# When a head's queries and keys are made ready: always ahead, or when their products are there

## The chip, the cores and the metric

One Trainium2 chip, one of its NeuronCores. The metric is device time in microseconds, the median of several executions of the same program.

## The reference, cut to what matters

Two transformer blocks, one after the other, on 512 tokens of width 1024. The first block is a feed-forward layer, a mixer, another feed-forward layer and a gated embedding; the second is a mixer with sparse attention and a mixture of 32 experts. The change lies in the first block's mixer, which has two kinds of attention side by side:

```python
u = rms_norm(h, g_mix[i]) @ w_in[i]
q_lat, kv_lat, k_rope, qd, kd, vd = jnp.split(u, IN_OFFSETS, axis=-1)
# diff_mixer, 4 heads, each with two pairs of q and k of width 64
q = rms_norm(qd.reshape(B, S, DIFF_HEADS, 2, DIFF_QK), g_q)
k = rms_norm(kd.reshape(B, S, DIFF_HEADS, 2, DIFF_QK), g_k)
a = a1 - lam * a2          # two softmaxes with a bias by distance
o = rms_norm(a @ v, g_sub) * (1.0 - lambda_init)
# mla_mixer, 8 heads: q and k come from normed latents by w_q_up and w_kv_up
h = h + jnp.concatenate([o_mla, o_diff], axis=-1) @ w_out[i]
```

## The kernel before

The program is written with a tile framework that adds waits and buffers. Products of the large weights are made with operands split in a high and a low half, three matmuls for one (lines 399 to 401; lines 651 to 653 where tokens stand on the partitions). A weight comes by a DMA of SP's queue; ScalarE writes its high half (line 376), VectorE or, for every other weight, GpSimd its low half (lines 379 and 383).

In the mixer of the first block two Python generators issue instructions in turns. `stream(tasks)` goes through the projections in the order of `TASKS1`: `qk1 v0 kv qk2 v1 ql0 ql1 rq qk3 kr ple0 rkv wkv krn mk mq0 mv ple1 mq1 wo2 wo3 wo0`. (`qk0` stands ahead of it.) `qk` makes the queries and keys of a diff head with their norms, `v` the values of two heads, `mk` and `mq` those of the MLA heads, `wo` is a quarter of the output projection, which waits for two finished heads, and `ple` belongs to the gated embedding. `attention()` goes through eight items in the order of `ITEMS1`: the diff heads d0 to d3, then the MLA pairs of heads m0 to m3. For each there are four steps:

- `prep` (`diff_n`, `mla_n`): TensorE turns the normed products (line 836), and ScalarE, VectorE and, for MLA, GpSimd write the high and low halves of queries and keys (lines 391 to 395, `dq`, `dk`, `mq`, `kt`). It first waits with `need` until the products are marked as there.
- `score` (`diff_s`, `mla_s`): score matmuls (line 414 for d, 399 to 401 for m), the row's extreme on VectorE (860, 962), exponentials on ScalarE (864, 964); for d, VectorE joins the two softmaxes (873, tile `ad`).
- `out` (`diff_o`, `mla_o`): TensorE turns the probabilities (1153), ScalarE or VectorE copies them (1155, 1157), and they are multiplied by the values (884, 986).
- `diff_f` for d: the last norm of a head's output (line 905).

`score` of a head is issued in turns with `out` of the head before it. Before the loop, two heads are made ready; inside it, each turn makes ready the head two ahead, gathered in `late`.

`merge` decides whose turn it is. Each `yield` of a generator names a cost, and `merge` keeps a sum for each, `t[0]` for attention and `t[1]` for tasks; `self.clock` follows the tasks' sum. With the weights `wa` and `wb` of the call, here 100.0 and 135.0:

```python
i = 0 if t[0] * w[1] <= t[1] * w[0] else 1
if g[i] is None or blocked == i and g[1 - i] is not None:
    i = 1 - i
```

A `yield None` (a `need` that isn't met) hands the turn to the other. A product is there at the clock of its `mark` plus a lag, 8.0 (`LAG`) for normed products and 1.0 for values. The costs sum to 137.9 for the tasks (a block of `qk` or `v` 11.2, `mq` 5.6, `mk` and `mv` 2.8, a projection 5.2, a `wo` 10.4) and to 99.6 for attention.

The order in which the generators issue is an order of priority: when the program is built, a scheduler can put a later instruction of an engine in front of one that it takes to be still waiting. On the chip each engine then keeps to the order that came out.

Of the kernel before, what the change touches and what calls it, by code (L numbers as in the profile page):

```python
# [28 lines left out]
NWM = 32  # L29
LAG = 8.0  # L30
ITEMS1 = "d0 d1 d2 d3 m0 m1 m2 m3"
TASKS1 = "qk1 v0 kv qk2 v1 ql0 ql1 rq qk3 kr ple0 rkv wkv krn mk mq0 mv ple1 mq1 wo2 wo3 wo0"
TASKS2 = "qi1 qi2 qi3 qa0 ka0 va0 qa1 ka1 va1 qa2 ka2 va2 qa3 ka3 va3 ckv qb0 ukv qb1 qb2 qb3 g00 g01 g02 g03 g04 g05 g06 g07 u00 u01 u02 u03 g10 g11 g12 g13 g14 g15 g16 g17"
LK, LQ, LA, LB = 1.0, 9.0, 3.0, 0.0
# [202 lines left out]
class Prog:  # L237
# [329 lines left out]
    def block1(self):  # L567
# [45 lines left out]
        done = {}  # L613
# [16 lines left out]
        def mark(key, lag=0.0):  # L630
            done[key] = self.clock + lag
# [39 lines left out]
        def evac(t, b, ps):  # L671
            with self.tc.high_priority(offset=HP1):
                for i in (0, 1):
                    c = slice(256 * i, 256 * i + 256)
                    nc.scalar.activation(t[:, c], ps[:, c], AF.Copy, scale=rx[0][:, 2 * b + i : 2 * b + i + 1])
# [21 lines left out]
        def values(v):  # L697
            def then(b, ps):
                t = self.U("vd")
                evac(t, b, ps)  # L700
                for h in (2 * v, 2 * v + 1):
                    for i in (0, 1):
                        vd[h, 2 * b + i] = t[:, 256 * i + P * (h % 2) : 256 * i + P * (h % 2) + P]
                    mark(("v", h), 1.0)
            return then

        rx = []
# [95 lines left out]
        def t_ple(w, half):  # L803
            for m4 in range(4):
                ps = self.G()
                self.gemm(ps, w, pT, 2, o=m4 * 256)
                y = self.U("pp")
                nc.scalar.copy(y, ps)
                self.sumsq(accp, y, len(pp) == 0)
                pp.append(y)  # L810
                yield 1.3
# [90 lines left out]
        def diff_f(h):  # L902
            y, rr = M_.pop(("f", h))
            t = self.U("on")
            nc.vector.scalar_tensor_tensor(t, y, gs[:, 3:4], self.bc1(rr), op0=OP.mult, op1=OP.mult)
            oT[4 + h] = self.HL(f"oT{4 + h}")
            self.split(oT[4 + h], t)
            yield 0.4
# [107 lines left out]
        for b in range(2):  # L1016
            T_[f"ple{b}"] = [(I["w_pp"][b], lambda w, b=b: t_ple(w, b))]
        tasks = sum((T_[n] for n in TASKS1.split()), [])
        score, out, prep = {"d": diff_s, "m": mla_s}, {"d": diff_o, "m": mla_o}, {"d": diff_n, "m": mla_n}

        def attention():
            items = [(n[0], int(n[1])) for n in ITEMS1.split()]
            fin = []
            late = []
            for kind, i in items[:2]:
                yield from prep[kind](i)
            for n, (kind, i) in enumerate(items):
                g = [score[kind](i)]
                if n:
                    g.append(out[items[n - 1][0]](items[n - 1][1]))  # L1030
                yield from self.zip_(*g)
                if fin:
                    yield from diff_f(fin.pop())
                if n and items[n - 1][0] == "d":
                    fin.append(items[n - 1][1])

                late += items[n + 2 : n + 3]
                if late and (late[0][0] == items[n + 1][0] or kind != items[n + 1][0] or len(late) > 1):
                    while late:
                        k2, i2 = late.pop(0)  # L1040
                        yield from prep[k2](i2)
            yield from out[kind](i)

        for _ in self.stream(lead):
            pass
        self.merge(attention(), self.stream(tasks), 100.0, 135.0)
        self.dump("oT", [t[:, 0, :].bitcast(F32) for t in oT])
        acc3 = self.U("acc3")
        xs = []
# [1207 lines left out]
```

## Time and profile before

| | |
|---|---|
| median of 3 runs | 2174.3 us (2173.36 to 2177.2) |
| the profiled execution, its own time | 2175.46 us |
| its span, first to last instruction | 2173.6 us |
| TensorE busy (PE) | 2094.4 us, 96% |
| weight loads of TensorE (PEld) | 1513.4 us, 70% |
| VectorE (DVE) | 949.0 us, 44% |
| ScalarE (ACT) | 734.7 us, 34% |
| GpSimd (POOL) | 536.6 us, 25% |
| mean granted clock of TensorE | 0.983 |

Busy is the share of the span in which an engine executes. PEclk is the granted clock of TensorE: 1.00 is 2.4 GHz, 0.50 is 1.2 GHz, and a value between them is a mean over a stretch with both. In a timeline row the bracket tells how long the engine had been idle and what it waited for. The matmuls overlap, so one lasts longer in a row than it is apart from the next.

### The profile page before, as it was taken

Reading aid. Unit: us, or ns where it says so; the run is one execution under the profiler, and the core shown is the slowest. Engines: PE = TensorE matmul, PEld = TensorE weight load, DVE = VectorE, ACT = ScalarE, POOL = GpSimd, SP = SyncE. Lnnn points to the kernel's source line nnn. Section 1 sums busy time; section 2 is a strip of 40 time slices with the busy share of each in tenths; the row PEclk is TensorE's granted clock in tenths of the full one; section 3 lists DMA queues with packets and bytes.
Section 4 is the critical chain, followed back from the end, with each engine's and each line's share of the span. In section 5 each row is a group of like instructions: output and inputs, shape, how many; then the busy total and the mean of one; then the engine's idle time right before and its main releaser. Section 6 shows DMA issues by size and latency. Waiting matters only on the chain.

```text
span 2173.6 us, 26063 instructions
## 1 busy us (share of the span) xinstructions
PE 2094.4 (96%) x10321; PEld 1513.4 (70%) x10321; DVE 949.0 (44%) x1671; ACT 734.7 (34%) x1233; POOL 536.6 (25%) x441
## 2 busy tenths in 40 slices
PE   8999999998799999999998999999999999999997
PEld 6888888875566788888877777667887455545544
DVE  4323234555565532332476995553253232323322
ACT  4213223444663422222443667442231111111112
POOL 3323234221520532323443445111230000000000
PEclk9999999999799999999999999999999999999999
DMA  4333333320101233333322101012626899999994
GB/s 162 97 94 92 96 97 107 119 69 30 39 20 38 79 98 97 97 97 97 103 89 78 49 30 54 30 46 71 230 69 243 353 398 415 420 409 406 416 395 161
DMA packets 67984, 331.01 MB, mean 152 GB/s; under 512 B 7808, under 2 KB 8976, under 8 KB 43792
## 3 DMA queue, kind: packets, MB, share of 16 engines
q1 hardware_dynamic: 67280, 328.24, 41.0%
q8 instruction: 83, 1.36, 0.3%
q10 hardware_dynamic: 576, 1.05, 0.1%
q14 instruction: 45, 0.37, 0.1%
HBM read 327.16 MB, written 2.10 MB: 151 GB/s over the span
## 4 chain that ended last, share of the span: by engine, by line
PE 82%; DVE 7%; ACT 5%; POOL 2%; issue 2%; DMA 0%; SPq 0%; DVEq 0%; ACTq 0%; POOLq 0%
PE pss L1820 10%; PE psg L399 9%; PE psg L401 9%; PE psg L400 9%; PE psg L1820 8%; PE pss L401 4%; PE pss L399 4%; PE pss L400 4%; PE pst L400 4%; PE pst L399 4%; PE pst L401 4%; PE pst L1820 4%; ACT whl L376 1%; PE psg L651 1%; PE psg L653 1%
## 5 line engine op out<-in xcount | busy, mean ns | idle before, releaser
L383 POOL TENSOR_TENSOR whl<-wraw,whl 128x512 fp32r<-128x512 f32 x228 | 304.3, 1356 | 626.8 <-ACT whl L376 414.5
L376 ACT ACTIVATE whl<-wraw 128x1024 fp32r<-128x1024 f32 (+1 forms) x227 | 237.0, 1045 | 618.7 <-PE psg L401 241.1
L379 DVE TENSOR_TENSOR whl<-wraw,whl 128x1024 fp32r<-128x1024 f32 (+1 forms) x113 | 156.9, 1388 | 64.2 <-ACT whl L376 64.0
L2120 POOL TENSOR_TENSOR fr<-fv,mhalf 128x1 f32<-128x1 f32 x4 | 2.2, 545 | 513.8 <-DVE fv L2119 512.1
L1820 PE MATMUL pss<-mw,xe 128*64 128x512 f32 x512 | 115.3, 592 | 0.0
L1820 PE MATMUL pss<-mw,hT 128*64 128x512 f32 x480 | 109.7, 611 | 0.6 <-ACT hT L1998 0.5
L1820 PE MATMUL psg<-mw,xe 128*64 128x512 f32 x480 | 108.2, 593 | 0.0
L524 POOL TENSOR_TENSOR t<-t,t 128x512 f32<-128x512 f32 x44 | 57.3, 1302 | 202.1 <-DVE t L523 189.7
L523 DVE TENSOR_TENSOR t<-pss,rb_f 128x512 f32<-128x512 f32 x44 | 30.4, 691 | 162.9 <-PE pss L401 162.9
L556 DVE SCALAR_TENSOR_TENSOR h<-pst,h 128x512 f32<-128x512 f32 x48 | 33.2, 692 | 140.2 <-PE pst L401 140.2
L2093 DVE TENSOR_TENSOR h<-h,psg 128x512 f32<-128x512 f32 x120 | 81.2, 687 | 22.8 <-PE psg L1820 22.8
L1980 DVE SCALAR_TENSOR_TENSOR mt<-pss,sc,mt 128x512 f32<-128x512 f32 x16 | 12.0, 751 | 179.1 <-PE pss L1820 178.5
L1820 PEld LDWEIGHTS pss<-mw,xe 128*64 128x64 f32 x512 | 36.7, 137 | 73.1 <-issue 73.1
L1820 PEld LDWEIGHTS psg<-mw,xe 128*64 128x64 f32 x480 | 34.4, 137 | 68.1 <-issue 64.8
L1820 PEld LDWEIGHTS pss<-mw,hT 128*64 128x64 f32 x480 | 33.9, 140 | 65.1 <-issue 61.1
L395 DVE SCALAR_TENSOR_TENSOR yel<-pss,sc,yeh 128x512 fp32r<-128x512 f32 x32 | 24.0, 751 | 121.5 <-ACT yeh L394 121.5
L1820 PE MATMUL pst<-disp,uhh 128*128 128x256 f32 x256 | 66.7, 287 | 1.2 <-DVE disp L1898 1.2
L521 DVE TENSOR_TENSOR t<-psg,rb_f 128x512 f32<-128x512 f32 x44 | 30.4, 691 | 81.6 <-PE psg L401 76.1
L1820 PE MATMUL pst<-disp,uhl 128*128 128x256 f32 x256 | 65.2, 281 | 0.0
L1979 ACT ACTIVATE mt<-psg,sc 128x512 f32<-128x512 f32 x16 | 11.0, 687 | 157.1 <-PE psg L1820 134.2
L394 ACT ACTIVATE yeh<-pss,sc 128x512 fp32r<-128x512 f32 x32 | 22.0, 687 | 115.2 <-PE pss L1820 105.0
L433 POOL TENSOR_TENSOR acc<-acc,sq 128x512 f32<-128x512 f32 x33 | 49.9, 1513 | 39.8 <-ACT sq L432 36.3
(938 smaller groups left out, 5693.8 us busy)
## 6 DMA issues: line engine op xcount, KB each, us to landing
mw<-in_w SPq DMA_DIRECT2D x188, 1024.0 KB, 9.4
wraw<-in_w_gu SPq DMA_DIRECT2D x87, 512.0 KB, 3.6
wraw<-in_w_d SPq DMA_DIRECT2D x48, 512.0 KB, 3.5
wraw<-in_w2A SPq DMA_DIRECT2D x38, 512.0 KB, 3.5
wraw<-in_w_inB SPq DMA_DIRECT2D x12, 512.0 KB, 3.5
wraw<-in_w_out SPq DMA_DIRECT2D x8, 512.0 KB, 3.5
wraw<-in_w_pg SPq DMA_DIRECT2D x8, 512.0 KB, 3.5
wraw<-in_w_up SPq DMA_DIRECT2D x8, 512.0 KB, 3.4
```

The source lines that it names most:

```text
L376: nc.scalar.activation(hl[:, 0, :n], raw[:, :n], AF.Copy)
L379: nc.vector.tensor_sub(hl[:, 1, :n], raw[:, :n], hl[:, 0, :n].bitcast(F32))
L383: nc.gpsimd.tensor_sub(hl[:, 1, c], raw[:, c], hl[:, 0, c].bitcast(F32))
L399: mm(ps, whi, xhi, start=first, stop=False)
L400: mm(ps, whi, xlo, start=False, stop=False)
L401: mm(ps, wlo, xhi, start=False, stop=last)
L433: (eng or nc.gpsimd).tensor_add(acc, acc, t)
L521: nc.vector.tensor_tensor(t1, pg, rb, op=OP.mult)
L524: nc.gpsimd.tensor_tensor(t2, t1, t2, op=OP.mult)
L556: nc.vector.scalar_tensor_tensor(self.h[m], py, 0.5, self.h[m], op0=OP.mult, op1=OP.add)
L1820: return self.next_to(nc.tensor.matmul(*args, **kw))
L2093: self.nc.vector.tensor_tensor(self.h[m], self.h[m], ps, op=OP.add)
```

## The change

The loop of `attention()` is written anew. Only the first head is made ready before it. In a turn, where the head to be scored isn't ready yet, it is made ready then, followed by a `yield` of the new constant `GAP`, 2.5, which issues nothing; in the first turn, head 1 is made ready too if its products are there. At the end of a turn, heads up to two ahead are made ready, but only while `there` says that their products are marked and due by the clock. `there` asks and doesn't wait. The weights of `merge` become 118.0 and 138.0. `values` marks the values of its two heads when its second half is issued, no longer after the first half too.

```diff
--- before.py
+++ after.py
@@ -29,6 +29,7 @@
 NWM = 32
 LAG = 8.0
 ITEMS1 = "d0 d1 d2 d3 m0 m1 m2 m3"
+GAP = 2.5
 TASKS1 = "qk1 v0 kv qk2 v1 ql0 ql1 rq qk3 kr ple0 rkv wkv krn mk mq0 mv ple1 mq1 wo2 wo3 wo0"
 TASKS2 = "qi1 qi2 qi3 qa0 ka0 va0 qa1 ka1 va1 qa2 ka2 va2 qa3 ka3 va3 ckv qb0 ukv qb1 qb2 qb3 g00 g01 g02 g03 g04 g05 g06 g07 u00 u01 u02 u03 g10 g11 g12 g13 g14 g15 g16 g17"
 LK, LQ, LA, LB = 1.0, 9.0, 3.0, 0.0
@@ -701,7 +702,8 @@
                 for h in (2 * v, 2 * v + 1):
                     for i in (0, 1):
                         vd[h, 2 * b + i] = t[:, 256 * i + P * (h % 2) : 256 * i + P * (h % 2) + P]
-                    mark(("v", h), 1.0)
+                    if b:
+                        mark(("v", h), 1.0)
             return then
 
         rx = []
@@ -1021,10 +1023,26 @@
         def attention():
             items = [(n[0], int(n[1])) for n in ITEMS1.split()]
             fin = []
-            late = []
-            for kind, i in items[:2]:
+            rope = [True]
+
+            def there(kind, i):
+                return all(key in done and self.clock >= done[key] for key in ([("qk", i)] if kind == "d" else ["mk", ("mq", i // 2)]))
+
+            def ready(kind, i):
                 yield from prep[kind](i)
+
+            yield from ready(*items[0])
+            made = 1
             for n, (kind, i) in enumerate(items):
+
+
+                if made == n:
+                    yield from ready(*items[n])
+                    made += 1
+                    yield GAP
+                elif n == 0 and there(*items[1]):
+                    yield from ready(*items[1])
+                    made += 1
                 g = [score[kind](i)]
                 if n:
                     g.append(out[items[n - 1][0]](items[n - 1][1]))
@@ -1033,17 +1051,14 @@
                     yield from diff_f(fin.pop())
                 if n and items[n - 1][0] == "d":
                     fin.append(items[n - 1][1])
-
-                late += items[n + 2 : n + 3]
-                if late and (late[0][0] == items[n + 1][0] or kind != items[n + 1][0] or len(late) > 1):
-                    while late:
-                        k2, i2 = late.pop(0)
-                        yield from prep[k2](i2)
+                while made < min(n + 3, len(items)) and there(*items[made]):
+                    yield from ready(*items[made])
+                    made += 1
             yield from out[kind](i)
 
         for _ in self.stream(lead):
             pass
-        self.merge(attention(), self.stream(tasks), 100.0, 135.0)
+        self.merge(attention(), self.stream(tasks), 118.0, 138.0)
         self.dump("oT", [t[:, 0, :].bitcast(F32) for t in oT])
         acc3 = self.U("acc3")
         xs = []
```

## Rows read from the trace of the kernel before

**Rows 1.** The page: busy times, and TensorE in 40 slices of the span.

```profile
PE 2094.4 (96%) x10321; PEld 1513.4 (70%) x10321; DVE 949.0 (44%) x1671; ACT 734.7 (34%) x1233; POOL 536.6 (25%) x441
PE   8999999998799999999998999999999999999997
```

**Rows 2.** Busy time by stage: us, engines (count), PEclk, DMA.

```profile
405.04:417.30 12.26, 12.26 (x107) 12.26 (x106) 5.22 (x10) 5.79 (x11) 2.56 (x2) 1.00 0.25 87
417.30:431.87 14.57, 14.35 (x83) 10.62 (x81) 10.01 (x33) 8.01 (x16) 2.54 (x2) 1.00 0.21 72
431.87:451.77 19.90, 19.90 (x169) 19.90 (x168) 10.25 (x22) 10.64 (x21) 5.10 (x4) 1.00 0.24 81
451.77:478.85 27.08, 26.59 (x139) 19.22 (x137) 18.63 (x55) 15.17 (x32) 2.73 (x3) 1.00 0.15 44
505.81:528.86 23.05, 17.09 (x77) 9.78 (x76) 14.08 (x50) 11.13 (x27) 1.27 (x1) 0.90 0.05 18
528.86:549.98 21.12, 14.49 (x54) 7.61 (x53) 14.56 (x48) 9.56 (x23) 2.69 (x3) 0.82 0.09 26
549.98:575.22 25.24, 20.89 (x71) 16.26 (x72) 10.37 (x26) 17.06 (x32) 9.25 (x8) 0.70 0.00 0
621.76:640.17 18.41, 17.54 (x94) 11.41 (x93) 13.65 (x24) 9.05 (x22) 2.51 (x2) 1.00 0.06 22
640.17:661.10 20.93, 17.88 (x95) 11.97 (x94) 12.62 (x20) 12.44 (x28) 5.40 (x4) 0.92 0.00 0
```

**Rows 3.** The fourth stage, line 651 alone, then line 401 alone.

```profile
451.77:478.85 27.08, 2.56 (x9) 1.70 (x9) 1.00 0.15 44
451.77:478.85 27.08, 6.63 (x16) 3.02 (x16) 1.00 0.15 44
```

**Rows 4.** The same columns in two shorter stretches.

```profile
524.00:528.00 4.00, 2.67 (x11) 1.76 (x9) 1.03 (x3) 1.33 (x4) 0.00 (x0) 0.52 0.00 0
548.00:560.00 12.00, 10.57 (x36) 8.34 (x35) 4.96 (x15) 4.46 (x9) 4.06 (x4) 0.50 0.00 1
```

**Rows 5.** Timeline of TensorE: start us, us, what, [idle before].

```profile
427.08 0.40 PE L401 MATMUL psg<-xs2h,whl 128*128 128x512 f32 x1
429.40 0.40 PE L399 MATMUL psg<-xs6h,whl 128*128 128x512 f32 x1
451.77 1.04 PE L836 MATMUL pst<-ident,y 128*128 128x128 f32 x8
505.81 1.03 PE L836 MATMUL pst<-ident,y 128*128 128x128 f32 x8
513.84 0.50 PE L414 MATMUL pss<-dkh,dqh 64*128 64x512 f32 x1 [1.06 <-DVE mn L860]
521.87 0.49 PE L414 MATMUL pss<-dkh,dqh 64*128 64x512 f32 x1 [1.57 <-DVE mn L860]
547.23 2.08 PE L884 MATMUL psg<-at,vd 128*128 128x512 f32 x2 [5.52 <-ACT at L1155]
587.00 1.33 PE L836 MATMUL pst<-ident,ym 128*128 128x128 f32 x5 [1.17 <-DVE ym L668]
594.17 0.50 PE L401 MATMUL pss<-kth,mql 128*128 128x512 f32 x1 [1.74 <-POOL mql L392]
621.76 1.28 PE L836 MATMUL pst<-ident,ym 128*128 128x128 f32 x8
```

**Rows 6.** Timeline of VectorE and GpSimd.

```profile
508.41 0.75 DVE L395 SCALAR_TENSOR_TENSOR dkl<-pst,g,dkh 128x512 fp32r<-128x512 f32 x1 [0.35 <-ACT dkh L394]
512.42 0.75 DVE L873 SCALAR_TENSOR_TENSOR ad<-sb,cf 128x512 f32<-128x512 f32 x1
541.97 2.49 POOL L383 TENSOR_TENSOR whl<-wraw,whl 128x512 fp32r<-128x512 f32 x2 [10.38 <-ACT whl L376]
543.29 1.72 DVE L873 SCALAR_TENSOR_TENSOR ad<-sb,cf 128x512 f32<-128x512 f32 x1
625.75 2.51 POOL L392 TENSOR_TENSOR mql<-mqn,mqh 128x512 fp32r<-128x512 f32 x2 [9.12 <-ACT mqh L391]
```

## The prediction

> **What bounds the kernel now.** I read the page first: TensorE is busy 96% of the span, no other engine half of it, and its 40 slices stand at 9 but for a dip in the tenth and eleventh (489 to 598 us) [rows 1]. That dip is the first block's attention, which is all the change touches; before and behind it only time moves. I then cut this stretch by stages [rows 2]. The reader is to see two kinds. In the dense kind (405 to 479 us) VectorE and ScalarE are half busy, and whenever a score waits, projection matmuls stand ready: in the 27.08 us from 451.77 TensorE idles 0.49. In the sparse kind the same attention work stands with hardly anything beside it: from 505.81 TensorE idles 5.96 of 23.05, from 528.86 6.63 of 21.12, from 549.98 4.35 of 25.24, with a granted clock down to 0.70 [rows 2]. So the limit is local: TensorE's own work in one place, a chain through VectorE and ScalarE in the other. The timeline of TensorE shows that chain: score pairs at 513.84 and 521.87 with one pair between, 4.0 us a pair, each having waited for VectorE's L860 [rows 5].
>
> Call one head's scores with the outputs of the head before it a bundle. Walking through the merge's arithmetic with the code's costs gives the order of before, and the trace agrees. d0's scores alone and then d1's with d0's outputs stand in the dense place (417 and 452 us); at tasks' time 80.4, when d3's products come due, two bundles stand one behind the other (505.81 and 528.86): d2 with d1's outputs, d3 with d2's. The cause is the loop: it wants head n+1 made ready before head n is scored, so all scores stand one head late, behind the wait for products.
>
> **What the change does to the order.** The same walk with the new loop: d0's scores go to task time 8.4 instead of 19.6; d1's scores and d0's outputs to 19.6 and 23.7 instead of 47.2; d2 with d1's outputs to 47.2 instead of 80.4; only d3 with d2's outputs stays at 80.4. At 101.1, m0 is scored after its own preparation alone; m1's preparation comes behind that bundle, and m1's bundle now before mq1 and wo2, not behind them. m2 is prepared at 115.8 and scored at once, as is m3. The later marking of v costs nothing: it keeps d0's outputs from asking for values not issued yet.
>
> The pause gives no cover. A pause adds 2.5 to attention's time, and tasks come next only if that then exceeds 118/138 of theirs. At the five pauses (task times 19.6, 47.2, 80.4, 101.1, 115.8) the allowance is 16.8, 40.4, 68.7, 86.4, 99.0; attention stands at 7.3, 19.5, 32.1, 45.1, 75.3 behind the pause. It is never ahead. The new ratio binds first in m3's bundle, at 99.0, and the old one did there too (85.8). I cost pause and ratio at nothing; were there cover, it would be tasks between preparation and score.
>
> **The sum.** *Sparse place.* Two bundles and the last 12 ple0 matmuls take 505.81 to 549.98, 44.17 us [rows 2]. One remains. From above, the first bundle's 23.05 plus the 12 matmuls uncovered: ten stand 2.32 us apart end to end [rows 5], 0.232 each, 2.8, so 25.9. From the other side, the second bundle's 21.12, which held these 12, plus the preparation chain no longer done ahead, from the transposes at 505.81 to the end of the last low half at 508.41 + 0.75 = 509.16 [rows 5, 6], 3.35, so 24.5. I take 25.2: saved 19.0.
>
> *Dense place.* The bundle moved there costs what a bundle costs among projections. The stage from 451.77 holds one, with 9 matmuls of line 651, which is a third of its kind (lines 651 to 653), and 16 of line 401, a third of its own (399 to 401) [rows 3]: 27 and 48. The former stand 19.90/169 = 0.118 apart [rows 2]. So 27.08 - 27 x 0.118 - 48 x 0.232 - 1.04 for the transposes of a preparation [rows 5] = 11.7, plus 0.5 for half as many transposes in d0's finish, which moves too: 12.2. Cover is there for the waits of d1 and d2 on their fresh halves; without it each would cost up to 3.35. Net of both places: -6.8.
>
> *MLA heads.* Preparation in a join between two bundles is dearer than behind tasks: the stage from 640.17, with m3's preparation, idles 3.05, the one from 621.76, with m2's behind mq1 and wo2, 0.87 [rows 2]. There will be two such joins (m1, m3) instead of one: +2.2. m1's 12 transposes leave the half-clock place, where five took 1.33 (0.27 each), for one where eight take 1.04 (0.13) [rows 5]: -1.6. Then m1, m2 and m3 are scored at once, and the first score may wait for its low halves. From below 0, since the outputs of the head before fill in; from above the whole chain, 621.76 to the second mql at 628.26, 6.5 less 1.0 of transposes, 5.5 [rows 5, 6]. The one such wait shown, m0's, is 1.74 with GpSimd loaded [rows 5]; there GpSimd is busy only 2.5 to 5.4 us in some 20 [rows 2]. I take 0.6 each: +1.8. Together +2.4.
>
> *Clock.* At the end of the first sparse bundle the granted clock is 0.52 and from 548 to 560 us 0.50 [rows 4], the lower level of 1.2 GHz, after a wait of 5.52 on a ScalarE copy [rows 5]. The 10.57 us of matmuls there would take 5.3 less at 2.4 GHz. That is the upper bound of a gain if the chain behind is entered warm, nothing the lower: the first bundle too ended cold. I take 1.6.
>
> Preparing fewer heads ahead shortens the lives of tiles; no stage shows a wait for one, so nothing for that. DMA is busy 0.25 or less [rows 2]: nothing either. Sum: -6.8 + 2.4 - 1.6 = -6.0. The profiled execution took 2175.46 us (2173.6 of span and 1.9 around it), so 2169.5; it stands 1.2 above the median 2174.3, so 2168.3 as a median.
>
> One rule speaks against it. At 541.97 GpSimd splits a weight, and VectorE's `ad` at 543.29, beside it, takes 1.72 against 0.75 elsewhere [rows 6]. The Trainium skill (SBUF — State Buffer, section "SBUF: two separate sides") says that VectorE with two SBUF inputs and GpSimd take turns on one pair of ports, each for a whole instruction, and the trace agrees with its 1.72. By the row alone it is late once; by the rule every split that meets such an instruction does this.
>
> **Rivals.**
>
> *Fresh heads wait (the other side).* m1, m2 and m3 stop TensorE for their low halves, as m0 does at 594.17. At 4 us each, in the upper part of the bounds, that is 12 instead of 1.8: +4.2, 2178.5. It cancels the gain at 2.6 us each. For it: the pause places nothing between. Against it: 16 transposes and their output products of the head before are ready. 15 in 100.
>
> *The dense place is not free.* The moved bundle goes at its chain's 4.0 us a pair, 16 us instead of 12.2, because projection evacuations queue on ScalarE behind exponentials. Then -2.2, 2172.1, which would count as no change. For it: two bundles stand nearer there. Against it: 0.49 idle in the stage from 451.77. 25 in 100.
>
> *More than the sum.* The waits of the fresh heads vanish and the chain behind the sparse place runs warm: -6.8 + 0.6 - 5.3 = -11.5, 2162.8. 15 in 100.
>
> *Ports.* Eight weight splits stand in 405 to 452 us (2, 2 and 4) [rows 2]; if each meets the moved bundle's VectorE work and holds it 0.97 us uncovered, +7.8, so +1.8, 2176.1. Against it: TensorE is full there. 5 in 100.
>
> The sum itself has 40 in 100, with a range of its own of 2165.5 to 2171.
>
> **Numbers.** 0.2%, 4.3 us, is about what a measurement of this kernel can tell from no change. Faster: three quarters of the sum's 40, the 15 of more, 5 of the dense rival's: 0.50. Same: 10, 18 and 4 of the ports: 0.32. Slower: the 15 of the fresh heads and 3 over: 0.18. The range reaches from below the larger gain, 2161, to 2177, short of the fresh heads' time.
>
> **What would show it.** In the changed profile: one bundle between the last kr projection and the first kvlh matmul, which come 17 to 21 us closer together; stages before it longer by about 12 us and still full; GpSimd's mql as releaser of scores of m1 to m3, under 1 us each. Wrong if TensorE idles in the early stages, if the sparse place loses less than 15, or if the MLA stretch grows by over 6.

## The result, and the profile after

The changed kernel takes 2192.44 us (2191.54 to 2193.55, 4 runs) beside 2174.01 of the kernel before in the same series: a ratio of 1.0082, 95% interval 1.0065 to 1.0100. It is slower by 18.4 us, where 2168.3 was forecast, and lies outside the range. The profiled execution took 2193.55 us, its span is 2191.8.

Line numbers after are one higher in the helpers, two higher in the task code and 15 higher behind `attention()`: L860 is L862, L884 is L886, L836 is L838, L401 is L402, L1155 is L1170.

The page first: the busy line and TensorE's slices, to stand beside [rows 1].

```profile
PE 2104.9 (96%) x10321; PEld 1518.6 (69%) x10321; DVE 952.5 (43%) x1671; ACT 735.7 (34%) x1233; POOL 537.3 (25%) x441
PE   8999999988689999999999899999999999999998
```

TensorE executes the same 10321 matmuls and is busy 10.5 us longer, at a mean granted clock of 0.978 beside 0.983, so part of the loss is a slower clock. The dip, 87 in the tenth and eleventh slice before, is now 8868 from the ninth, which begins at 438 us and was full.

Next, three stretches in the windows view, of equal work in both kernels but for a few matmuls at the first edge (under 0.5 us): from 405 to the norm of the q latents, which ends the dense place (L442 before, L443 after, the matmul on `accq`); from there to the first `mk` matmul that waits for `ym`, the sparse place; from there to the norm that opens the next feed-forward layer, the MLA heads. Before:

```profile
405.00:484.87 79.87, 75.91 (x513) 64.61 (x511) 47.22 (x122) 42.31 (x84) 17.55 (x14) 1.00 0.21 69
...
484.87:565.28 80.41, 63.32 (x290) 44.67 (x290) 39.80 (x123) 36.31 (x78) 13.93 (x13) 0.83 0.09 31
...
565.28:731.03 165.75, 153.01 (x720) 110.96 (x721) 107.83 (x166) 95.64 (x186) 58.62 (x43) 0.96 0.12 39
```

After:

```profile
405.00:511.76 106.76, 93.96 (x570) 73.66 (x568) 61.00 (x172) 51.70 (x107) 17.71 (x15) 0.92 0.17 52
...
511.76:571.64 59.88, 47.27 (x230) 35.87 (x230) 26.31 (x73) 26.80 (x55) 13.74 (x12) 0.82 0.12 41
...
571.64:748.62 176.98, 158.53 (x720) 112.75 (x721) 111.65 (x166) 96.22 (x186) 58.85 (x43) 0.94 0.12 36
```

The sparse place gives back 80.41 - 59.88 = 20.5 us, as forecast. The dense place costs 26.9 instead of 12.2, the MLA heads 11.2 instead of 2.4. Net +17.6, nearly all of the 18.2 between the spans.

Where the dense place loses is plain in one window of after, 20 us of the places that were full before [rows 2]:

```profile
432.00:452.00 20.00, 11.82 (x44) 6.25 (x44) 12.47 (x45) 8.71 (x21) 2.53 (x2) 0.66 0.10 30
```

TensorE is idle 8.18 of 20 us there, and what it does runs mostly at 1.2 GHz (0.66). Its timeline names the waits:

```profile
425.43 0.28 PE L654 MATMUL psg<-whl,xs3h 128*128 128x256 f32 x1
...
438.22 0.79 PE L415 MATMUL pss<-dkh,dqh 64*128 64x512 f32 x1 [2.25 <-DVE mn L862]
441.82 0.79 PE L415 MATMUL pss<-dkh,dqh 64*128 64x512 f32 x1 [1.95 <-DVE mn L862]
447.45 3.78 PE L886 MATMUL psg<-at,vd 128*128 128x512 f32 x4 [3.98 <-DVE mn L865]
452.03 0.36 PE L652 MATMUL psg<-whl,xs0h 128*128 128x256 f32 x1
```

This is d1's bundle on its own chain: a new sparse place, the same kind that the change took away behind 505. The next projection, qk2, starts at 452.03 only. Its weight can't be the reason: ScalarE wrote the high half at 432.18, and GpSimd had the low half done at 435.8. ScalarE's timeline shows what was late:

```profile
424.10 0.82 ACT L676 ACTIVATE y<-psg,r_mix 128x256 f32<-128x256 f32 x2
...
430.80 0.69 ACT L395 ACTIVATE dqh<-pst,gd 128x512 fp32r<-128x512 f32 x1 [3.33 <-PE pst L838]
...
434.85 0.72 ACT L866 ACTIVATE sb<-sb,mn 128x512 f32<-128x512 f32 x1 [1.61 <-DVE mn L865]
...
438.39 0.72 ACT L866 ACTIVATE sb<-sb,mn 128x512 f32<-128x512 f32 x1 [1.93 <-DVE mn L865]
...
442.05 0.72 ACT L866 ACTIVATE sb<-sb,mn 128x512 f32<-128x512 f32 x1 [1.99 <-DVE mn L865]
442.67 0.19 ACT L866 ACTIVATION_READ_ACCUMULATOR sb<-sb,mn 128x1 f32 x1
442.77 0.82 ACT L676 ACTIVATE vd<-psg,r_mix 128x256 f32<-128x256 f32 x2
```

The matmuls of v0's second half end with the row at 425.43; their evacuation stands at 442.77, behind five of d1's exponentials, three of which waited 1.6 to 2 us for VectorE. The kv latents' evacuation, on VectorE (L629), comes at 452.49. Projections share three PSUM buffers (`psg`): v0's half holds one, kv another, and d0's outputs take the third. That is a reason for qk2 to be late until v0's buffer is free, at 443.59, and not for the 8.4 us from there to 452.03: qk2 then stands behind d0's first outputs in TensorE's order, and these wait 3.98 us. Their first copy stands on VectorE behind the last pair of d1's scores:

```profile
446.70 0.69 DVE L1172 COPY at<-pst 128x512 f32<-128x512 f32 x1
```

In the MLA heads, [rows 5] had a wait of 1.74 before m0's first score. The same view after:

```profile
601.62 0.80 PE L402 MATMUL pss<-kth,mql 128*128 128x512 f32 x1 [2.96 <-POOL mql L393]
...
615.38 3.08 PE L838 MATMUL pst<-ident,ym 128*128 128x128 f32 x12
...
655.88 0.79 PE L1168 MATMUL pst<-ident,am 128*128 128x128 f32 x4 [2.02 <-DVE mqn L945]
...
678.72 0.50 PE L402 MATMUL pss<-kth,mql 128*128 128x512 f32 x1 [1.60 <-POOL mql L393]
```

m0 waits 2.96 and m3 1.60 for GpSimd's low halves. The 2.02 belong to m2's preparation: m1's transposes wait for VectorE, which reads m2's turned queries. m1's twelve transposes at 615.38 take 3.08, or 0.26 each, the price of the slow clock.

### The profile page after: what moved, and what is told of

Read it like the earlier page. It is cut to its first block, busy times and chain, and to the rows that moved or that the text cites. A ratio compares the mean times of both kernels' runs of the same rounds, so it can differ in the third digit from the quotient of the medians.

```text
span 2191.8 us, 26064 instructions
## 1 busy us (share of the span) xinstructions
PE 2104.9 (96%) x10321; PEld 1518.6 (69%) x10321; DVE 952.5 (43%) x1671; ACT 735.7 (34%) x1233; POOL 537.3 (25%) x441
## 4 chain that ended last, share of the span: by engine, by line
PE 84%; DVE 7%; ACT 4%; POOL 3%; issue 2%; DMA 0%; SPq 0%; DVEq 0%; ACTq 0%; POOLq 0%
PE pss L1835 10%; PE psg L400 9%; PE psg L402 9%; PE psg L401 9%; PE psg L1835 8%; PE pss L402 4%; PE pss L400 4%; PE pss L401 4%; PE pst L400 4%; PE pst L401 4%; PE pst L402 4%; PE pst L1835 4%; PE pss L415 1%; PE psg L654 1%; PE psg L653 1%
```

## The experiments

In each, "as before" means the old order of that kind of head, and a difference is against the median of the kernel before in the same series (2173.1 to 2174.7). Theory A: the loss is in two places that add, d1's bundle in the dense place and the MLA heads scored on fresh halves. Rivals: it is all in the MLA heads, or in the pause and the weights.

**1. No pause, old weights**

```diff
-GAP = 2.5
+GAP = 0.0
-        self.merge(attention(), self.stream(tasks), 118.0, 138.0)
+        self.merge(attention(), self.stream(tasks), 100.0, 135.0)
```

> The changed kernel with the pause at 0 and the merge weights back at 100 and 135. By the merge's arithmetic neither ever gives a task a turn before the last heads: the same time as the changed kernel, 2192.4 within 0.2% (2188 to 2197). If pause and ratio carry the loss, it falls back towards 2174.

2190.38 us, ratio 1.0077 (1.0061 to 1.0094): +16.1. Pause and weights don't carry the loss.

**2. Diff heads as changed, MLA heads as before**

```diff
-                while made < min(n + 3, len(items)) and there(*items[made]):
+                while made < min(n + 3, len(items)) and (n > 2 if items[made][0] == "m" else there(*items[made])):
```

> The new order for the diff heads alone; the MLA heads are made ready as before (m0 and m1 behind d3, then m2 and m3 two ahead). From the stages of the two traces the diff part moved the time by 26.9 up to the last qk stage and by 20.6 back in the sparse place, so theory A (the diff part's early place costs more than it was worth) expects about +7, 2179 to 2184. Theory B (the loss lies in MLA heads scored fresh) expects the forecast's -6.8 for this part, about 2167.

2181.42 us, 1.0035 (1.0022 to 1.0047): as theory A expects.

**3. Diff heads as before, MLA heads as changed**

```diff
-            made = 1
+            yield from ready(*items[1])
+            made = 2
...
-                while made < min(n + 3, len(items)) and there(*items[made]):
+                while made < min(n + 3, len(items)) and (items[made][0] == "d" or there(*items[made])):
```

> The old order for the diff heads, the new one for the MLA heads. From the stages of the two traces the MLA stretch got about 10 us longer: theory A expects 2182 to 2187 here (its share beside that of the diff part, the two adding up to 18). Theory B expects the whole 18 here, 2192. The forecast's own term would give 2176.4.

2189.29 us, 1.0071 (1.0054 to 1.0088): above theory A's range and below theory B's 2192. The parts sum to 22.1, more than the 18.4 of the whole. Both kept the new weights, which with one part alone leave more output projections (`wo`) bare behind the last head: in the program's order 108 and 120 such matmuls, against 66 before and 78 after. So both were run again with the edit of 1, which makes it 66:

**4. As 2, no pause, old weights**

> As the second experiment (new order of the diff heads, MLA heads as before), but with the pause at 0 and the weights 100 and 135, so that 66 output-projection matmuls are left behind the last head, as in the kernel before; the second experiment left 108 there. Theory A expects the diff part's share alone, about +5.5 by its stages: 2178 to 2181. If the 42 matmuls that stood bare cost nothing, the time stays at the second experiment's 2181.4; if they cost 0.1 us each, 2177.

2180.04 us, 1.0028 (1.0019 to 1.0038): +5.3.

**5. As 3, no pause, old weights**

> As the third experiment (old order of the diff heads, new one of the MLA heads), with pause 0 and weights 100 and 135: 66 matmuls behind the last head instead of 120. Theory A expects the MLA share alone, 10 to 12: 2184 to 2187. The forecast's term for it was +2.4, 2176.7.

2186.44 us, 1.0057 (1.0039 to 1.0075): +11.7. The parts sum to 17.0 beside the 16.1 of run 1: theory A stands, and the rival with everything in the MLA heads falls. The next six runs take the diff part apart.

**6. d0 and d1 held apart, in the changed kernel**

```diff
             for n, (kind, i) in enumerate(items):
+                while n == 0 and not there(*items[1]) or n == 1 and self.clock < 31.0:
+                    yield None
```

> The changed kernel, but d0 is scored where it was before (when d1's products are due, task time 19.6, d1 made ready with it) and d1's bundle waits for task time 31, so that evacuations and norms of qk1, v0 and kv are issued ahead of it. Theory A in its sharper form (the bundle itself costs 12.2 among projections; the other 14.7 are evacuations queued on ScalarE and VectorE behind the early exponentials, which hold the projections' PSUM banks) expects 2192.4 - 14.7, about 2178, with 2174 to 2182 allowed. Its rival, that a second bundle in this place costs 27 wherever in it it stands, expects 2192.

2182.80 us, 1.0035 (1.0021 to 1.0050): 10.0 of the 18.4 came back, less than expected, and the time lies just outside the allowed range. The dense stretch shows why: it is still 18.4 us longer than before (98.30 beside 79.87), so the bundle itself costs more than 12.2:

```profile
405.00:503.30 98.30, 91.42 (x564) 73.72 (x562) 60.32 (x172) 50.77 (x107) 17.67 (x15) 0.97 0.18 55
```

**7. The same with MLA heads as before, no pause, old weights**

> d0 scored where it was before, d1's bundle held until task time 31 (as in the fourth experiment), MLA heads as before, pause 0, weights 100 and 135. By the stages of the fourth experiment its diff part ends 1.6 us earlier than in the kernel before; with no loss at the MLA heads theory A expects 2172 to 2174, level with or just under the kernel before. If the loss of the MLA stretch came from the diff part's order, it stays near 2182.

2172.94 us, 0.9995 (0.9985 to 1.0006): level, as expected. (What its expectation calls the fourth experiment is run 6 here.) It moves two bundles, so each was moved alone from run 4.

**8. d0 alone held**

```diff
+                while n == 0 and self.clock < 11.3:
+                    yield None
```

> The diff part alone (MLA heads as before, no pause, weights 100 and 135; it took 2180.0, 5.3 over before), with d0's scores held until the tasks' clock is 11.3, when qk1's block is issued; d1 is scored as early as in the change. Theory (evacuations behind exponentials): qk1's evacuation is ahead of d0's exponentials again, v0's second half and kv's stay behind those of d1; half of the loss comes back, 2176 to 2178. Rival (two bundles too near each other, whatever stands in ScalarE's queue): the bundles come nearer still, 2180 to 2182.

2181.41 us, 1.0041 (1.0028 to 1.0055): the theory's number missed, and the rival's came. I had also blamed qk1's evacuation, late at 424.10 in after; here ScalarE does it at 409.09, and nothing comes back. v0's half still stands at 443.01, and the window is as empty as in after:

```profile
432.00:452.00 20.00, 11.55 (x41) 6.54 (x41) 12.66 (x42) 8.41 (x20) 2.48 (x2) 0.74 0.12 35
```

**9. d1 alone held, until 31.0**

```diff
+                while n == 1 and self.clock < 31.0:
+                    yield None
```

> The diff part alone (2180.0), with d1's scores held until the tasks' clock is 31.0; d0 is scored as early as in the change. Theory: v0's second half is evacuated ahead of d1's exponentials, qk1's still behind those of d0; the other half or more of the loss comes back, 2174 to 2177. Rival (qk1's evacuation alone carries the loss): 2180.

2170.28 us (2167.68 to 2171.89, 11 runs), 0.9987 (0.9978 to 0.9996): better than the theory asked, and 2.8 us below the kernel before, the one version here whose interval lies under 1, though by less than the 0.2% that the prediction took as the least to be told. Its windows:

```profile
405.00:502.27 97.27, 90.66 (x577) 71.94 (x575) 60.42 (x173) 50.96 (x107) 18.15 (x15) 1.00 0.19 57
502.27:562.16 59.89, 47.30 (x229) 35.83 (x229) 26.31 (x73) 26.80 (x55) 13.73 (x12) 0.82 0.13 42
432.00:452.00 20.00, 20.00 (x132) 15.15 (x131) 11.93 (x39) 9.03 (x19) 3.00 (x2) 1.00 0.14 44
```

The 20 us are full. But a bundle moved by 11.4 of the tasks' clock also stands farther from d0's; the next two runs tell distance from queue.

**10. d1 held until 22.5**

As 9, with 22.5 for 31.0.

> The diff part alone with d1's scores held until the tasks' clock is 22.5 instead of 31.0: 2.9 later than in the change, 8.5 earlier than in the run that gave the loss back (2170.3). On ScalarE v0's second half stands ahead of d1's exponentials, as with 31.0. Theory (v0's evacuation queued behind exponentials holds TensorE's banks): most of the loss is back, 2171 to 2174, and TensorE is full from 432 to 452. Rival (the two bundles stand too near each other): about a quarter of the way from 2180 to 2170, 2177 to 2179.

2172.97 us, 0.9994 (0.9985 to 1.0003): level. d1 comes only 2.9 later than in run 4, just behind v0's block, and some 6 to 7 us are back. ScalarE's timeline shows v0's evacuations, now in one row with the first half's last block:

```profile
426.82 1.21 ACT L676 ACTIVATE vd<-psg,r_mix 128x256 f32<-128x256 f32 x3
```

The window of the 20 us:

```profile
432.00:452.00 20.00, 18.16 (x106) 12.41 (x104) 12.78 (x45) 9.47 (x21) 2.52 (x2) 1.00 0.14 49
```

And TensorE's timeline, qk2's first matmul:

```profile
440.23 0.36 PE L652 MATMUL psg<-whl,xs0h 128*128 128x256 f32 x1
```

v0's half leaves PSUM by 428.0 instead of 443.59, qk2 starts at 440.23, inside d1's bundle, and the granted clock is 1.00. kv's evacuation, on VectorE's timeline, is as late as in after:

```profile
452.78 0.68 DVE L629 TENSOR_TENSOR y<-psg,rb_mix 128x512 f32<-128x512 f32 x1
```

So kv's buffer isn't the one that counts; v0's may be. But the run moves something else with it. d0's first copy, in after behind the fourth pair of d1's scores, here stands behind the first, and qk2 again follows the outputs that it feeds:

```profile
438.17 0.69 DVE L1172 COPY at<-pst 128x512 f32<-128x512 f32 x1
```

In the changed kernel and in runs 4 and 8 both are late, v0's evacuation at 441 to 443 and the copy behind d1's last pair; in runs 6, 7 and 9 to 11 both are early. No run parts the two.

**11. d1 held until 39.0**

As 9, with 39.0.

> The diff part alone with d1's scores held until 39.0, behind qk2's block: more distance to d0, and qk2's evacuations ahead of d1's exponentials too, but d2's bundle comes nearer. Theory of the queue: nothing more to gain, 2169 to 2173. Rival of the distance: 2166 to 2169, since the 2.0 of waits that the run with 31.0 shows behind d0's outputs go too.

2172.38 us, 0.9996 (0.9987 to 1.0005): more distance gives nothing more, and that rival falls. What d1's bundle is put ahead of is left. The last four runs are on the MLA part.

**12. m1's bundle behind mq1, in run 1's kernel**

```diff
+                while n == 5 and not there(*items[6]):
+                    yield None
```

> The changed kernel with pause 0 and weights 100 and 135 (2190.4 in the first experiment), but m1's bundle waits until m2's products are due, so that it stands behind mq1 and wo2 again; m2 and m3 are then made ready ahead of their bundles. Theory C (what the MLA part costs is that m1's and m2's joins lose the cover of mq1 and wo2 and that m2 and m3 are scored fresh) expects the share of the MLA heads to go but for m0: 2190.4 - 8 = 2182, 2180 to 2184. Its rival, that the cost sits at m0 (a wait of 2.96 on GpSimd and half clock behind it), expects 2188 or more.

2185.44 us, 1.0054 (1.0035 to 1.0073): 5 of run 1's 16.1 back, not the 8 expected, and the two intervals overlap. The edit moves m1's bundle and also makes m2 and m3 ready ahead, so it can't tell which of these counts. The MLA stretch of run 1, then of this run:

```profile
570.95:747.05 176.10, 158.43 (x719) 112.62 (x720) 110.82 (x166) 96.33 (x186) 59.11 (x43) 0.94 0.12 36
...
572.24:744.07 171.83, 154.38 (x719) 110.90 (x720) 109.79 (x166) 95.49 (x186) 58.78 (x43) 0.95 0.12 37
```

Nearly all that comes back is busy time: 4.05 us, beside 0.22 of idle.

**13. As 5, with real turns behind a late preparation**

```diff
-                    yield GAP
+                    till = self.clock + 2.5
+                    while self.clock < till:
+                        yield None
```

> The MLA part alone (2186.4, 11.7 over before), but each head made ready late then hands its turns to the tasks until their clock has gone on by 2.5: about 24 task matmuls really stand between preparation and first score of m0 and m1 (m2 and m3 too while tasks are left). Theory (the first scores wait for fresh halves): the waits on GpSimd's mql before m0 and m1 fall under 1 us and the time to 2181 to 2184. Rival (the loss is in the joins that lost mq1 and wo2, which this doesn't give back): 2186.

2179.24 us, 1.0027 (1.0016 to 1.0038): +6.2, more than expected came back. The wait before m0's first score is gone, m1's is 0.50, m2's 1.30.

**14. As 5, with m1 made ready together with m0**

```diff
                     made += 1
-                    yield GAP
+                    if n == 4:
+                        yield from ready(*items[5])
+                        made += 1
```

> The MLA part alone (2186.4), but m1 is made ready together with m0, as before the change; m1's bundle still stands ahead of mq1, and m2 and m3 are still scored straight after their preparation. Theory: m1's 12 transposes and first score move out of a join; the stage of m0 and d3 is as before (2.8 back) and 1 to 2 more, 2182 to 2184. Rival (order of m1's bundle and mq1 is all): 2186.

2179.21 us, 1.0024 (1.0015 to 1.0033): +6.2, again more than expected. m0 waits 1.85.

**15. The edits of 13 and 14 together**

> The MLA part alone, with m1 made ready together with m0 and 2.5 of tasks really between late preparations and their scores. If the two edits give back different waits (m1's transposes and preparation in a join; the wait of a first score on fresh halves), they add up: 2174 to 2176. If both give back the same (m0's and m1's first score), 2178 to 2180, and the rest is m1 ahead of mq1 with m2 and m3 fresh.

2175.23 us, 1.0009 (1.0000 to 1.0018): +1.6, at the upper edge of what can be told from none. The edits add up. The windows of the MLA stretch show it, beside 165.75 us and 153.01 busy before. Run 5:

```profile
566.25:742.89 176.64, 158.39 (x719) 112.64 (x720) 110.88 (x166) 96.11 (x186) 58.95 (x43) 0.93 0.12 36
```

Run 13:

```profile
565.19:735.72 170.53, 155.74 (x720) 110.08 (x721) 108.08 (x166) 95.90 (x186) 58.97 (x43) 0.96 0.11 38
```

Run 14:

```profile
565.80:735.48 169.68, 154.27 (x719) 111.46 (x720) 108.52 (x166) 96.28 (x186) 58.48 (x43) 0.95 0.13 38
```

Run 15:

```profile
565.71:730.63 164.92, 152.47 (x719) 109.18 (x720) 107.49 (x166) 95.54 (x186) 58.63 (x43) 0.97 0.13 39
```

Of run 5's 10.9 us over before, 5.4 are longer busy time for the same matmuls (158.39 - 153.01) and 5.5 idle. Both go in run 15. m0 waits 2.57 in run 5, and a queue is part of the reason again, as the timelines of ScalarE and GpSimd show:

```profile
589.28 0.63 ACT L392 ACTIVATE mqh<-mqn 128x512 fp32r<-128x512 f32 x1 [2.21 <-DVE mqn L945]
...
587.34 2.96 POOL L384 TENSOR_TENSOR whl<-wraw,whl 128x512 fp32r<-128x512 f32 x2
590.26 3.60 POOL L434 TENSOR_TENSOR accp<-accp,sq 128x512 f32<-128x512 f32 x2
593.81 2.50 POOL L393 TENSOR_TENSOR mql<-mqn,mqh 128x512 fp32r<-128x512 f32 x2
```

A weight split and two sums of squares, 6.5 us in all, stand ahead of m0's `mql`, which starts 3.9 us behind the end of its high half. Before, GpSimd had the same three there (586.36 to 592.89), but m1's transposes stood on TensorE in front of the waiting score, and the wait was 1.74.

## Why the prediction was wrong

**The dense place is the step that failed first.** The sum put 12.2 on the argument that "cover is there", since projection matmuls had stood ready whenever a score waited [rows 2]. The rows were right about the old order: there, v0's second half was evacuated at 434.79 with d1's scores still 17 us off. The argument carried them to another order without asking whether the cover could still start. By the windows above the 26.9 are 18.05 of busy time (93.96 - 75.91) and 8.84 of idle. With d1 held (run 9) it is 14.75 busy at full clock and 2.65 idle, 17.4 in all. So my 12.2 was 2.55 short for the bundle's own work and took its 2.65 of idle at nothing; the other 9.5, 6.2 idle and 3.3 of longer busy time at a clock of 0.92 instead of 1.00, belong to the new sparse place. Runs 9 to 11 show what makes it: d1's bundle ahead of v0's second half. Behind it the cover starts in time. What in that order holds the cover up stays open between v0's evacuation behind d1's exponentials and d0's outputs behind d1's scores. The forecast had put the later mark of v, for which d0's outputs wait, at nothing; no run changes it alone.

The rival "The dense place is not free" had the right kind of mechanism, work queued behind the chain, and mis-sized it. I priced a late evacuation as a slower bundle, 4.0 us a pair or 16 in all. In fact the cover itself is gone, qk2 starting only at 452.03, and the clock falls with it. The condition to look for wasn't how near two bundles stand (run 11) but what the new chain is put ahead of (run 10).

The Trainium skill (PSUM — Partial Sum Buffer, section "Engine vs sequencer instructions") says that the queues of ScalarE, VectorE and GpSimd are strictly first in, first out. The trace agrees: of the 17.1 us between v0's last matmul and its evacuation ScalarE is idle 8.9, waiting in front of d1's preparation and exponentials with v0's product ready behind them. The Trainium skill (Perfetto Trace Analysis, section "Matmuls") also wants independent groups of matmuls to rotate through PSUM banks so that evacuations overlap the next group. In run 10, where v0's evacuation overlaps kv's matmuls, the time is 6 to 7 us less than in run 4, where it doesn't; how much of that is the evacuation's no run shows.

**The sparse place was right**, in its mechanism too: one bundle is left there, 19.0 was forecast and 20.5 measured, and run 9's trace repeats it (59.89 us).

**The MLA heads are the second failure**: +2.4 forecast, 11.7 alone (run 5). By the windows after, the 11.2 are 5.7 of idle and 5.5 of longer busy time, and for the second half the sum had no term here. Taken term by term:
- Joins, +2.2: not shown by itself. Run 15, with m1 made ready together with m0, takes one of the two joins away again; its stretch is 164.92 us, 0.8 less than before.
- m1's transposes, -1.6 for leaving the half-clock place: nothing of it came. They took 0.26 each at 615.38, no less than the 0.27 of [rows 5]. Moving m1's whole preparation back gave 5.6 to 7.2 us (run 14). The part that shows as a wait is small: m0 waits 1.85 instead of the 2.57 of run 5, since m1's transposes stand in its wait. Of the 7.0 us in the windows 2.8 are idle and 4.1 busy time.
- Fresh halves, 0.6 each or +1.8: m1, m2 and m3 wait 0.50, 2.02 and 1.60, the second in its preparation. m0 wasn't counted though it too is now scored straight behind its own preparation; it waits 2.96, 1.2 more than before. Real turns gave back 5.5 to 7.2 (run 13). The rival "Fresh heads wait" came nearer in the total, with 12 for these waits, and by luck: none reaches its 4 us, and half of the loss is busy time. It took cover from the sixteen transposes of the head before; m2's 2.02 stand right in front of such transposes.

How much of the slow clock in this stretch follows from which wait no run separates.

**The clock, -1.6**: nothing came. The sparse place kept a mean of 0.82 against 0.83 before. The two new stalls, in the dense place and at m0, cost clock instead.

**Pause and weights** were right at nothing within about 2 us (run 1), and so was the reason, that attention is never ahead at a pause: in run 1 TensorE's order is that of the changed kernel up to m3's bundle at 686 us, where I saw the ratio bind first. What I didn't see is that turns that are really handed over are worth about 6 us to the MLA part (run 13). What the output projections left bare behind the last head cost isn't shown: the MLA stretch takes 166.22 us in run 2 and 166.21 in run 4, but 178.37 in run 3 and 176.64 in run 5, and the intervals of each pair overlap.

Of the signs I named, two came: TensorE idles in the early stages, and the MLA stretch grew by over 6. The ports show no part in it: after, fifteen of the sixteen `ad` took 0.75 and one, at 550.03, took 1.72.

## What to carry to other kernels

Before counting an idle stretch as covered by independent matmuls, check that these can still start: which buffers they write, when those are evacuated, and what stands ahead of them in each engine's order. A chain that waits a few us an item holds everything queued behind it. When work is moved into a full place, try it behind the evacuation of the last started product as well as ahead; here 2.9 of the tasks' clock were worth 6 to 7 us. Preparing a step early isn't only latency hiding: its instructions can fill a wait of the step ahead of it, as m1's transposes did for m0, and they are missed there when they move.

## What was not expected

With one bundle 2.9 of the tasks' clock too early, TensorE is idle 8 of 20 us in a place where it stood at 100%, and the granted clock falls from 1.00 to 0.66 with it; behind v0's block both come back (18.16 busy, 1.00). A half product stays in PSUM for 17 us on the way. And a GpSimd queue that is busy only a quarter of the span started two short instructions of a head 3.9 us late, behind 6.5 us of other work.
